# The swap of halves in a rotary embedding: from two half-height multiplies on VectorE to two ScalarE copies and one full multiply

## The chip, the cores and the metric

The kernel runs on one core of a Trainium2 chip. The metric is device time in microseconds (us) from one launch to its end. The core has five engines that run side by side: TensorE (PE) multiplies matrices, VectorE (DVE) and ScalarE (ACT) work element by element, GpSimd (POOL) here only issues DMAs, and SyncE (SP) issues most of the other DMAs. Each engine takes its instructions in a fixed order, which is decided when the program is built, and waits at each until its inputs are there.

## The reference

One layer of an encoder is applied to two sequences, x_sample with 1024 tokens and x_prompt with 512, each with 2048 channels, all in float32. The input is normalised and multiplied by one combined weight w_in. Of the columns of the result, three groups of 1024 feed a convolution path (value, gate inside the path, output gate); the rest are eight query heads, two key heads and two value heads of 128 channels and the attention's output gate. Queries and keys get a rotary embedding:

```python
t1, t2 = tf[..., :half], tf[..., half:]
out = jnp.concatenate([t1 * cos - t2 * sin, t2 * cos + t1 * sin], axis=-1)
```

Here `half` is 64. Then come a windowed attention with a sink term, the convolution (31 taps per channel, layer norm, silu, a 1024x1024 weight), the gates, one output weight, the residual and a last normalisation.

## The kernel before

Activations lie with the channels on the 128 partitions and the tokens along the free dimension, so one head of a projection is a tile of 128 partitions x 512 tokens, and the two halves of a head are partitions 0 to 63 and 64 to 127. Every product is taken in three passes with a high and a low part of each operand (`parts`, L506 to L515: ACT writes the high part, DVE the rest).

The long sequence is projected by `Unit` (L94 on), which takes two head-wide columns and two halves of the tokens at once in seven products of twelve matmuls instead of eight (a Strassen-like scheme). ACT copies the accumulator (`tap`, L236), DVE adds (L257), and the second half of the 2048 input channels is added to the stored first half by an accumulating DMA, which POOL issues (`add_into`, L501) and which lands in an SBUF tile. When it has landed, a generator finishes the tile: for queries and keys that is `rotate` (L1076), which calls `rope` in place on the tile. These generators stand in a list (`later`, L266) and are run some products later by `turn_over` (L542), behind the ACT and DVE instructions issued last before them and with a raised priority. There are 10 heads of queries and keys and two halves of the tokens, so 20 calls. Queries stand beside an attention gate column (L1240), whose tile gets a multiply (L975) and a Silu (L983) shortly before.

The short sequence is projected by plain `Job`s (L386), 48 matmuls each into one of four accumulators. Its rotations read the accumulator in PSUM directly (`rotated`, L1073), as the evacuation of the job, with a raised priority and in the middle of the next job: 10 calls. At the same time the attention of the long sequence runs in a lane of generators, PE, DVE and ACT by turns (L1151 to L1213).

The convolution's taps (L1033, L1041) run on DVE in another lane of generators, which is advanced after each product at a rate; they fill DVE between the urgent work. The final order on each engine comes from a planner, which takes the instruction of highest priority that it believes to be ready at that time.

`rope` (L1061 to L1071) uses a scratch tile `b`, from one of two rings of four buffers in turn (`E`, L477), and the tables `cos` and `sin` (`rope_tables`, L1052; for the long sequence multiplied once with the norm's factor). The result is stored to DRAM by SP (L1074, L1078; in the profile L504).

Of the kernel before, what the change touches and what calls it, by code (L numbers as in the profile page):

```python
# [9 lines left out]
AF = mybir.ActivationFunctionType  # L10
ALU = mybir.AluOpType
# [734 lines left out]
class Sequence:  # L746
# [314 lines left out]
    def rope(self, acc, c, o=None):  # L1061
        e, nc = self.e, self.e.nc
        i = slice(c * W, c * W + W)
        if o is None:
            o = e.G()
        b = e.E()
        nc.vector.tensor_tensor(b[0:64], acc[64:128], self.sin[64:128, i], ALU.mult)
        nc.vector.tensor_tensor(b[64:128], acc[0:64], self.sin[0:64, i], ALU.mult)
        nc.vector.tensor_tensor(o, acc, self.cos[:, i], ALU.mult)
        nc.vector.tensor_tensor(o, o, b, ALU.add)  # L1070
        return o  # L1071
# [1105 lines left out]
```

## Time and profile before

| what | value |
|---|---|
| median of three runs | 2080.51 us (2079.76 to 2081.54) |
| profiled execution, first to last instruction | 2072.4 us |
| median minus that span | 8.1 us |
| PE busy | 2057.6 us (99%) |
| DVE busy | 1752.3 us (85%) |
| ACT busy | 1043.9 us (50%) |
| first rotation of the long sequence starts | 642.0 us |
| last one of the long sequence starts | 830.0 us |
| rotations of the short sequence start | 871.1 to 1021.6 us |
| calls of `rope` | 30 |

The profile is of one execution, and its times count from the first instruction. A row of a timeline holds the start, the duration, the engine, the line of the kernel, the operation, the tiles it writes and reads, and, in brackets, how long the engine stood idle before it and what ended that. A row of a group holds the number of instructions, then the busy time in us, the mean duration in ns, and the idle time ahead. PEld is the weight load of PE; an engine name with a q is that engine's queue issuing a DMA. Tiles go by their ring's name: g and u are the rings of `E`, a, b and c are accumulators in PSUM, hl the split weights, raw the weights as loaded.

### The profile page before, as it was taken

To read this page: it belongs to the slowest core of one execution; us is meant where nothing else is said; L and a number is where in the kernel's file an instruction comes from. 1 tells how busy PE (TensorE), PEld (TensorE's weight loads), DVE (VectorE), ACT (ScalarE), POOL (GpSimd) and SP (SyncE) were. 2 spreads that over 40 slices of the span, in tenths; PEclk is the share of its full clock that TensorE was granted. 3 is DMA by queue.
4 is the path that set the end of the run, shared out by engine and by line. 5 is a ranking of instruction groups with operands and counts; after the bars stand their busy time and mean duration, and the time that the engine had idled before them with its cause. 6 is when DMAs were issued, how large, how long until landed. Compare 5 with 4: busy or idle time off the path is not lost.

```text
span 2072.4 us, 27195 instructions
## 1 busy us (share of the span) xinstructions
PE 2057.6 (99%) x9256; PEld 1696.0 (82%) x9256; DVE 1752.3 (85%) x2873; ACT 1043.9 (50%) x1711; POOL 157.8 (8%) x240
## 2 busy tenths in 40 slices
PE   9999999999999999999999999999999999999998
PEld 8888888888888888788888888888888888888886
DVE  8767899998899999889866877767799978998877
ACT  7485445333464443644455777336454343454454
POOL 0111111101111112100000000000000111100000
PEclk9999999999999999999999999999999999999999
DMA  8888786864577776954455555997789899678897
GB/s 295 312 299 254 197 222 220 292 214 154 193 242 192 178 173 172 290 169 154 159 172 187 176 183 182 317 331 235 246 288 302 281 317 297 206 249 297 290 334 275
DMA packets 242300, 494.56 MB, mean 239 GB/s; under 512 B 23664, under 2 KB 84464, under 8 KB 242160
## 3 DMA queue, kind: packets, MB, share of 16 engines
q1 hardware_dynamic: 216352, 428.83, 61.6%
q0 software_dynamic: 24512, 61.88, 12.1%
q10 hardware_dynamic: 1296, 2.11, 0.3%
q8 instruction: 72, 1.18, 0.2%
q14 instruction: 68, 0.56, 0.1%
HBM read 331.77 MB, written 160.96 MB: 238 GB/s over the span
## 4 chain that ended last, share of the span: by engine, by line
PE 52%; issue 7%; DVE 4%; DMA 2%; POOL 1%; ACT 1%; POOLq 0%; ACTq 0%; SPq 0%; DVEq 0%
PE a L670 14%; PE c L670 7%; PE b L670 7%; PE a L207 7%; PE c L207 3%; PE s L1168 2%; PE pv L1197 2%; PE s L1851 2%; PE a L1851 2%; PE b L207 1%; PE pt L1202 1%; DVE hl L511 1%; PE pt L1851 1%; PE pv L1851 1%; POOL u L501 1%
## 5 line engine op out<-in xcount | busy, mean ns | idle before, releaser
L207 PE MATMUL a<-t,hl 128*128 128x512 f32 x2640 | 633.1, 390 | 2.0 <-ACT g L236 1.3
L207 PEld LDWEIGHTS a<-t,hl 128*128 128x128 f32 x2640 | 493.2, 188 | 109.5 <-ACT g L236 2.6
L510 ACT ACTIVATE hl<-raw 128x1024 fp32r<-128x1024 f32 (+3 forms) x334 | 296.1, 890 | 375.3 <-PE c L207 90.6
L511 DVE TENSOR_TENSOR hl<-raw,hl 128x1024 fp32r<-128x1024 f32 (+3 forms) x334 | 337.9, 1012 | 143.6 <-ACT hl L510 142.0
L670 PE MATMUL a<-t,hl 128*128 128x512 f32 x1344 | 325.8, 393 | 0.0
L207 PE MATMUL c<-t,hl 128*128 128x512 f32 x1320 | 319.2, 389 | 0.0
L670 PEld LDWEIGHTS a<-t,hl 128*128 128x128 f32 x1344 | 248.9, 188 | 50.2
L207 PEld LDWEIGHTS c<-t,hl 128*128 128x128 f32 x1320 | 247.4, 188 | 51.5 <-DVE u L304 0.2
L1041 DVE SCALAR_TENSOR_TENSOR f<-f,c_w_dw,f 128x512 f32<-128x512 f32 x248 | 173.3, 745 | 0.3
L670 PE MATMUL b<-t,hl 128*128 128x512 f32 x672 | 163.6, 393 | 1.3 <-DVE t L515 0.8
L1004 DVE SCALAR_TENSOR_TENSOR f<-f,c_w_dw,f 128x512 f32<-128x512 f32 x232 | 163.7, 745 | 1.0 <-ACT f L999 0.9
L670 PE MATMUL c<-t,hl 128*128 128x512 f32 x672 | 164.4, 393 | 0.0
L207 PE MATMUL b<-t,hl 128*128 128x512 f32 x660 | 159.8, 389 | 0.0
L670 PEld LDWEIGHTS b<-t,hl 128*128 128x128 f32 x672 | 124.6, 188 | 27.4 <-DVE t L515 1.1
L670 PEld LDWEIGHTS c<-t,hl 128*128 128x128 f32 x672 | 124.7, 188 | 24.7
L207 PEld LDWEIGHTS b<-t,hl 128*128 128x128 f32 x660 | 123.7, 188 | 25.6
L1033 DVE SCALAR_TENSOR_TENSOR f<-f,w_both,f 128x512 f32<-128x512 f32 x120 | 89.8, 748 | 2.3 <-ACT f L1027 0.3
L236 ACT ACTIVATE u<-a 128x512 f32<-128x512 f32 x82 | 48.7, 594 | 69.7 <-PE a L207 66.9
L236 ACT ACTIVATE g<-a 128x512 f32<-128x512 f32 x78 | 46.4, 595 | 70.0 <-PE a L207 65.1
L1182 ACT ACTIVATE p<-p,tiny 128x384 f32<-128x384 f32 (+1 forms) x96 | 54.5, 570 | 44.1 <-DVE tiny L1179 25.2
L510 ACT ACTIVATE a<-pt 128x512 fp32r<-128x512 f32 x64 | 38.0, 593 | 63.9 <-PE pt L1202 63.6
L418 ACT ACTIVATE hl<-raw 128x1024 fp32r<-128x1024 f32 x43 | 45.4, 1056 | 47.1 <-PE a L670 18.7
(354 smaller groups left out, 2713.0 us busy)
## 6 DMA issues: line engine op xcount, KB each, us to landing
raw<-w_in SPq DMA_DIRECT2D x170, 512.0 KB, 5.2
raw<-w_out SPq DMA_DIRECT2D x31, 512.0 KB, 5.3
raw<-w_pw SPq DMA_DIRECT2D x24, 512.0 KB, 4.2
wsum_P<-raw SPq DMA_DIRECT2D x47, 256.0 KB, 3.5
raw<-wsum_P SPq DMA_DIRECT2D x18, 512.0 KB, 4.7
f<-x_s SPq DMA_DIRECT2D x16, 512.0 KB, 8.7
g<-wsum_P SPq DMA_DIRECT2D x28, 256.0 KB, 4.4
a<-sum_S SPq DMA_DIRECT2D x24, 256.0 KB, 6.7
```

The lines of the kernel that those rows point to most:

```text
L207: nc.tensor.matmul(acc, hl[:, l, o, j, :], toks[j][:, r], start=name in FRESH and j == 0 and q == 0, stop=name in LAST and j == HALF - 1 a ...
L236: nc.scalar.activation(t, bank, AF.Copy)
L418: e.nc.scalar.activation(t[:, 0], raw, AF.Copy)
L510: nc.scalar.activation(hi, x, AF.Copy)
L511: nc.vector.tensor_tensor(lo, x, hi.bitcast(F32), ALU.subtract)
L670: nc.tensor.matmul(job.acc[0], hl[:, l, kk // HALF, kk % HALF, :], r, start=i == 0 and p == 0, stop=i == nk - 1 and p == 2,)
L1004: nc.vector.scalar_tensor_tensor(t, h[:, j : j + T], w(j), t, ALU.mult, ALU.add)
L1033: nc.vector.scalar_tensor_tensor(m0, odd[:, j : j + H], both(j), m0, ALU.mult, ALU.add)
L1041: nc.vector.scalar_tensor_tensor(out, d[:, j : j + H], w(2 * j + k), out if j else m0, ALU.mult, ALU.add)
L1168: nc.tensor.matmul(ps[:, 0:n], qs[:, x, h], k[y][:, keys], start=p == 0, stop=p == 2)
L1182: nc.scalar.activation(p[:, 0:n], p[:, 0:n], AF.Exp, bias=nm[:, h : h + 1], accum_out=l[:, h : h + 1])
L1851: nc.tensor.matmul(acc[t], self.toks[name, m][:, x, i, t * P : (t + 1) * P], parts[i][l].rearrange("p a b -> p (a b)"), start=fresh and fi ...
```

## The change

The swapped product `b` was written by two DVE multiplies, each from one half of the tile to the other half of `b`. Now two ACT copies write the swapped halves, and one DVE multiply of all 128 partitions multiplies `b` in place by the sine table. Since the multiplier now is indexed by the output's half and not by the input's, the table's signs are exchanged. The cosine multiply and the addition stay.

```diff
         b = e.E()
-        nc.vector.tensor_tensor(b[0:64], acc[64:128], self.sin[64:128, i], ALU.mult)
-        nc.vector.tensor_tensor(b[64:128], acc[0:64], self.sin[0:64, i], ALU.mult)
+        nc.scalar.activation(b[0:64], acc[64:128], AF.Copy)
+        nc.scalar.activation(b[64:128], acc[0:64], AF.Copy)
+        nc.vector.tensor_tensor(b, b, self.sin[:, i], ALU.mult)
         nc.vector.tensor_tensor(o, acc, self.cos[:, i], ALU.mult)
         nc.vector.tensor_tensor(o, o, b, ALU.add)
...
-    arrays["sin"] = np.concatenate([sin, -sin])
+    arrays["sin"] = np.concatenate([-sin, sin])
```

## The prediction

> **What bounds the kernel now.** I read the page first: its span and the busy shares.
>
> ```profile
> span 2072.4 us, 27195 instructions
> PE 2057.6 (99%) x9256; PEld 1696.0 (82%) x9256; DVE 1752.3 (85%) x2873; ACT 1043.9 (50%) x1711; POOL 157.8 (8%) x240
> ```
>
> TensorE is without an instruction for 2072.4 - 2057.6 = 14.8 us in all, VectorE (DVE) for 320 us, ScalarE (ACT) for more than half of the span. A shared average can hide a stage, so next came busy time by stretches: one without rotary work, the 20 rotations of the long sequence (640 to 835 us), and the 10 of the short one (835 to 1026 us). The columns are PE, weight loads, DVE, ACT, POOL, each with its count of instructions, then clock, DMA share and GB/s.
>
> ```profile
> 400.00:620.00 220.00, 219.81 (x970) 181.69 (x969) 199.65 (x298) 95.09 (x145) 26.02 (x45) 1.00 0.63 209
> 640.00:835.00 195.00, 194.62 (x862) 159.71 (x861) 190.67 (x285) 78.14 (x122) 35.04 (x40) 1.00 0.71 175
> 835.00:1026.00 191.00, 188.59 (x875) 154.46 (x874) 171.60 (x302) 97.94 (x177) 6.08 (x7) 1.00 0.60 193
> ```
>
> Two things stand here. In 640 to 835 DVE has only 195.00 - 190.67 = 4.33 us left, so it is nearly full where the change acts. Yet PE misses only 0.38 us there, and its instructions come at 195.00 / 862 = 0.226 us, as they do with DVE at 91% (220.00 / 970 = 0.227 us). PE sets the pace; DVE is full because filler work (the convolution taps) is put into it. What the change can win on PE while it acts is at most 0.38 + 2.41 = 2.8 us of idle time.
>
> **What the change removes on DVE.** Grouped by shape within 640 to 835, then all calls of the first multiply by stretch:
>
> ```profile
> L1067 DVE TENSOR_TENSOR g<-u,f 64x512 f32<-64x512 f32 x10 | 6.9, 687 | 0.8 <-DMA u<-part_q 0.6
> L1068 DVE TENSOR_TENSOR g<-u,f 64x512 f32<-64x512 f32 x10 | 6.9, 685 | 0.1
> L1070 DVE TENSOR_TENSOR u<-u,g 128x512 f32<-128x512 f32 x10 | 6.9, 687 | 0.1
> ```
>
> ```profile
> 640.00:835.00 195.00, 13.73 (x20) 1.00 0.71 175
> 835.00:1026.00 191.00, 6.93 (x10) 1.00 0.60 193
> ```
>
> A multiply of 64 partitions takes 0.687 us, as long as one of 128 (0.687 us). Two go and one comes: 0.69 us of busy time per rotation, 20.6 us over 30. What an engine really pays is the distance between starts, and there the old pair costs more:
>
> ```profile
> 660.18 0.68 DVE L1070 TENSOR_TENSOR g<-g,u 128x512 f32<-128x512 f32 x1
> 660.79 0.68 DVE L257 TENSOR_TENSOR u<-g,u 128x512 f32<-128x512 f32 x1
> 661.39 0.68 DVE L143 TENSOR_TENSOR p<-raw,raw 128x512 f32<-128x512 f32 x1
> 662.11 0.69 DVE L1067 TENSOR_TENSOR g<-u,f 64x512 f32<-64x512 f32 x1
> 662.81 0.69 DVE L1068 TENSOR_TENSOR g<-u,f 64x512 f32<-64x512 f32 x1
> 663.52 0.69 DVE L257 TENSOR_TENSOR g<-c,g 128x512 f32<-128x512 f32 x1
> ```
>
> Full operations follow each other at 0.60 us. The one ahead of the pair, the first and the second half take 0.72, 0.70 and 0.71 us. From L143 to the next L257 pass 2.13 us; with one full multiply in place of the halves it would be 2 x 0.60 = 1.20. DVE wins 0.93 us per rotation: 18.6 us in 640 to 835, 9.3 us behind it, 27.9 us in all.
>
> The Trainium skill names the cause in "VectorE: DVE Perf Modes", section "Two Vector instructions with no wait between them": an operation whose input or output starts in another group of 32 partitions than the last one's is held until every earlier one has finished. The trace agrees (0.70 to 0.72 against 0.60 us). By durations alone the sum on DVE would be 20.6 us, by the rule 27.9 us; PE's time is the same by both.
>
> Worth on PE: bounds 0 and -2.8 us (all idle of both stretches). I take -0.2 us, half of the 0.38 us, because the cover of DVE's work is PE itself and the 2.41 us lie at the change of sequences (below), after the last long rotation.
>
> **What it adds on ACT.** No copy of 64 partitions is in the trace. Nearest are full 128x512 operations in the same stretch (from SBUF, SBUF, PSUM), and two back to back:
>
> ```profile
> L510 ACT ACTIVATE hl<-raw 128x512 fp32r<-128x512 f32 x20 | 12.5, 624 | 45.7 <-DVE raw L143 43.6 <-PE c L207 2.2
> L983 ACT ACTIVATE g<-g 128x512 f32<-128x512 f32 x9 | 5.7, 633 | 14.1 <-DVE g L975 14.1
> L236 ACT ACTIVATE u<-a 128x512 f32<-128x512 f32 x20 | 11.8, 589 | 5.6 <-PE a L207 5.4
> ```
>
> ```profile
> 848.03 0.63 ACT L983 ACTIVATE g<-g 128x512 f32<-128x512 f32 x1
> 848.55 0.62 ACT L983 ACTIVATE u<-u 128x512 f32<-128x512 f32 x1
> ```
>
> Lower bound per copy: half of 0.589, 0.29 us; upper: 0.633 + 0.10 if it were held as DVE's halves are, 0.73 us. I take 0.62, since halving the partitions won nothing on DVE. A pair then fills 0.52 + 0.62 = 1.14 us (bounds 0.6 and 1.5); 30 pairs are 34 us. ACT has 116.9 us free in the first stretch, 93.1 in the second. The question is what stands behind the copies on ACT. That is the evacuation of PE's accumulator (L236), and PE waits for it. The rotations come in pairs, one per half of the tokens. The last first-of-a-pair:
>
> ```profile
> 829.74 1.05 ACT L510 ACTIVATE hl<-raw 128x1024 fp32r<-128x1024 f32 x1
> 830.02 0.69 DVE L1067 TENSOR_TENSOR g<-u,f 64x512 f32<-64x512 f32 x1
> 830.96 2.88 PE L207 MATMUL c<-t,hl 128*128 128x512 f32 x12
> 831.15 0.60 ACT L236 ACTIVATE g<-a 128x512 f32<-128x512 f32 x1 [0.37 <-PE a L207]
> 833.67 0.61 PE L207 MATMUL a<-t,hl 128*128 128x512 f32 x2
> ```
>
> The copies can start at 830.7, when ACT is done with L510, and end near 831.9 at worst ahead of the evacuation, which then ends at 832.5 instead of 831.75. PE wants that bank at 833.67: 1.2 of 1.9 us of room are left, cost 0. Without this room each such rotation would cost up to 0.75 us. At the second of a pair ACT is empty; this is the evacuation's neighbour for the rotation that starts at 796.63:
>
> ```profile
> 798.86 0.63 ACT L510 ACTIVATE hl<-raw 128x512 fp32r<-128x512 f32 x1 [6.31 <-DVE raw L143]
> ```
>
> 6.31 us of idle ACT take 1.14 us at no cost. The copies also take over DVE's wait for the projection's accumulating DMA:
>
> ```profile
> DVE u L1067 <- DMA g<-part_q: 1.1, 1, 1.1
> DVE g L1067 <- DMA u<-part_q: 0.6, 1, 0.6
> ```
>
> Both are late second ones; 1.1 + 1.14 us is under the 6.31 us. In the short sequence the copies read PSUM (0.59 each) amid the attention's round trips, where PE's weight loads already wait shortly (620 to 1035 us):
>
> ```profile
> PEld pv L1197 <- DVE a L511: 1.3, 5, 0.4
> PEld pt L1202 <- ACT p L1189: 0.8, 3, 0.3
> ```
>
> That is 2.1 us in 8 waits, 0.26 each. Bounds for ten rotations: 0, and 10 x 1.14 = 11.4 us if each copy pair stood whole in a round trip. ACT is half empty there (97.94 of 191.00), so I take three of ten with one more such wait: +0.8 us.
>
> **What moves.** The full multiply waits for both copies, and the in-place cosine multiply of the long sequence too. Behind them on DVE the planner has other ready work, as it has now (L1041 stands between the parts of the rotation). The result was ready 3.5 us after the start (830.02 to 832.83 + 0.69); 1.14 + 0.60 + 0.60 + 0.69 is 3.0 us, plus handing over. So the store on SP's queue isn't later, and the weight load behind it has 6 us:
>
> ```profile
> 820.17 0.32 SPq L504 DMA_DIRECT2D q_d<-u  x1
> 826.31 0.33 SPq L127 DMA_DIRECT2D raw<-w_in  x1
> ```
>
> The tables' sign change is in the input and costs nothing; no DMA is added.
>
> **Sum.** -0.2 + 0 + 0.8 = +0.6 us on the profiled 2072.4, so 2073.0. The median of the runs is 2080.51, 8.1 above the span; with that, 2081.1 us.
>
> **Rivals.** *ACT blocks the evacuations* (slower). The trace has the mechanism once:
>
> ```profile
> 840.59 1.95 ACT L514 ACTIVATE t<-a,c_norm_g 128x512 fp32r<-128x512 f32 x3
> 842.44 0.58 ACT L236 ACTIVATE g<-a 128x512 f32<-128x512 f32 x1
> 843.07 3.01 PE L207 MATMUL a<-t,hl 128*128 128x512 f32 x12 [1.07 <-ACT g L236]
> ```
>
> 1.95 us of ACT ahead of an evacuation cost PE 1.07 us. Two copies behind one L510 are 1.14 + 1.05 = 2.19 us. It decides from four rotations on (4 x 1.07 = 4.3 us); with 8 of 20 it is +8.6, 2089 us. Against it: the 1.2 us of room above.
>
> *DVE's relief shows* (faster). DVE is 98% busy for 195 us, and if PE followed it, 18.6 + 9.3 us would go: 2052.6 us. Against it are the equal 0.226 and 0.227 us per PE instruction at 98 and 91% DVE. The Trainium skill, "Perfetto Trace Analysis", section "Identifying the Most-Contended Engine", distrusts PE's matmul busy share and would look at the weight loads, here 82%, which makes DVE the engine to relieve; the even spacing speaks against it here.
>
> *DVE stands waiting for the copies.* If nothing fills the 1.14 us, each rotation costs DVE 1.14 - 0.93 = 0.21 us more; 20 of them, 4.2 us, fit into the 4.33 us it has. Then the relief isn't there, and the time stays: 2080.5 to 2081.
>
> **Chances.** Forecast 0.65; ACT blocks 0.18; DVE's relief shows 0.07; DVE waits 0.10. The measurement can tell about 0.2%, 4.2 us. Within it fall the forecast and the last rival: same 0.75; faster 0.07; slower 0.18. The forecast's own range is -2.8 to +3 us, 2077.7 to 2083.5. For 8 in 10 I widen it upward into the blocking case, to 2088, and down to 2077; the planner orders everything anew, and moves waits of some tenths in later stages.
>
> **What would show it.** Right: DVE busy falls by about 20 us and what stands around the rotation on DVE follows at 0.60 us; copies take 0.6 us; PE's instructions in 640 to 835 still come at 0.226 us; PE's idle there stays under 1.5 us. Wrong: PE rows in these stretches with waits of 0.5 us and more on L236 or on L510, L1182 and L1189; ACT idle ahead of a copy with an evacuation ready behind it; or PE's spacing under 0.226 us, which would mean that DVE set it.

## The result, and the profile after

| what | value |
|---|---|
| changed kernel, median of 22 runs | 2077.62 us (2073.97 to 2081.12) |
| kernel before, 22 runs beside them | 2081.26 us (2076.56 to 2086.94) |
| ratio | 0.9981, 95% interval 0.9974 to 0.9988 |
| difference | -4.0 us (-5.4 to -2.5), from 0.0019 x 2081 |
| forecast | 2081.1 us, range 2077 to 2088 |

The change makes the kernel 0.19% faster. That is a gain, though a hair inside the 0.2% that the prediction called no change. The time lies in the range; the sign of the forecast (+0.6 us) is wrong.

The page of the changed kernel, its span and busy shares:

```profile
span 2077.4 us, 27223 instructions
PE 2060.1 (99%) x9256; PEld 1697.9 (82%) x9256; DVE 1728.4 (83%) x2843; ACT 1081.8 (52%) x1771; POOL 157.9 (8%) x240
```

This is a trap: the span after is 5.0 us *longer* than the 2072.4 us of before, though 22 runs say that the kernel is faster. The profiled execution of the changed kernel took 2079.13 us in all, 1.7 us more than its span, so about 1.7 us lie outside a span. The first profile of before would then be one of about 2074.1 us, below all 22 timed runs of that kernel. Both kernels were therefore profiled once more, for the comparisons below: the spans are then 2079.4 us (before) and 2073.8 us (after). One execution differs from the next by as much as the change is worth or more (7.0 us before, 3.6 us after), so a difference of two spans says nothing here. What two profiles of a kernel agree on can be used.

The stretches of the prediction, after (PE, weight loads, DVE, ACT, POOL, then clock, DMA share and GB/s):

```profile
640.00:835.00 195.00, 195.00 (x869) 160.99 (x868) 177.55 (x267) 104.78 (x162) 35.01 (x41) 1.00 0.74 177
835.00:1026.00 191.00, 189.20 (x879) 155.75 (x878) 163.76 (x291) 110.62 (x198) 6.00 (x7) 1.00 0.60 193
```

In the long sequence's rotations the stretch holds 869 instructions of PE where it held 862, and PE misses nothing. DVE's busy time falls by 190.67 - 177.55 = 13.1 us, which is 20 operations of 0.687 us (13.7 us). It is not free, though. The two longest of DVE's waits in this stretch after the change (total us, times, longest):

```profile
DVE u L1069 <- ACT u L1068: 7.1, 9, 1.6
DVE g L1069 <- ACT g L1068: 6.3, 4, 2.6
```

It stands 13.4 us at the new multiply (L1069 after the change), waiting for the second copy. Busy and waiting together are 177.55 + 13.4 = 191.0 us, as much as the 190.67 us before. The relief is eaten on DVE, and yet PE gains.

The copies, by shape from 640 to 1026 us, and one pair in the timeline (here and in the timelines below, rows of other work are left out):

```profile
L1068 ACT ACTIVATE g<-u 64x512 f32<-64x512 f32 x10 | 6.3, 632 | 0.1
...
L1068 ACT ACTIVATE g<-a 64x512 f32<-64x512 f32 x4 | 2.4, 592 | 0.1
```

```profile
789.36 0.63 ACT L1067 ACTIVATE g<-u 64x512 f32<-64x512 f32 x1
790.01 0.63 ACT L1068 ACTIVATE g<-u 64x512 f32<-64x512 f32 x1
790.66 0.60 ACT L236 ACTIVATE u<-c 128x512 f32<-128x512 f32 x1
790.67 0.69 DVE L1069 TENSOR_TENSOR g<-g,f 128x512 f32<-128x512 f32 x1
```

A copy of 64 partitions takes 0.632 us (0.592 in the short sequence, which reads PSUM). The two start 0.65 us apart, where two full operations before (848.03 and 848.55) started 0.52 apart. The last row but one is an evacuation that starts right behind the pair.

**Where PE's gain is.** The order of instructions on every engine is the same in both kernels up to about 641 us and again from about 1027 us. A steady difference must come from between. PE's own order is the same up to 938 us, so the same matmuls are compared. In all profiles I counted PE's instructions in 640 to 835 us: with the old pair 862 and 856 (two profiles of before), with the copies 869 and 868. The rows of the second profiles, before and after:

```profile
640.00:835.00 195.00, 194.15 (x856) 158.03 (x855) 189.16 (x283) 77.42 (x122) 35.03 (x40) 1.00 0.71 172
```

```profile
640.00:835.00 195.00, 195.00 (x868) 160.93 (x867) 177.91 (x269) 105.21 (x162) 35.69 (x41) 1.00 0.74 178
```

Of this count, 9.5 instructions more at 195 / 868.5 = 0.2245 us each are 2.1 us. PE's wait at 841 us (row 843.07 of the prediction) shrinks as well; PE's waits for the evacuation from 640 to 870 us, before and after:

```profile
PE a L207 <- ACT g L236: 1.3, 2, 1.1
...
PE a L207 <- ACT u L236: 0.2, 1, 0.2
```

```profile
...
PE a L207 <- ACT g L236: 0.3, 1, 0.3
```

The one at 841 us was 1.07 and 1.09 us in the two profiles of before, 0.35 and 0 in the two of after: on the mean some 0.9 us. Together 3.0 us, inside the interval of the difference. The way between two matmuls that are the same in all kernels, near 622 and near 843 us, gives as much: against the first profile of before, its second one takes 1.5 us more, the two of after 2.0 and 2.5 us less, 3.0 us on the mean.

**The mechanism.** At 826 us the same work stands in both timelines. Before:

```profile
825.00 2.88 PE L207 MATMUL c<-t,hl 128*128 128x512 f32 x12
826.20 0.68 DVE L975 TENSOR_TENSOR u<-u,f 128x512 f32<-128x512 f32 x1
826.91 0.64 ACT L983 ACTIVATE u<-u 128x512 f32<-128x512 f32 x1 [2.10 <-DVE u L975]
827.45 0.58 ACT L236 ACTIVATE u<-a 128x512 f32<-128x512 f32 x1
828.09 1.19 PE L207 MATMUL a<-t,hl 128*128 128x512 f32 x4 [0.20 <-ACT u L236]
```

After:

```profile
825.47 2.88 PE L207 MATMUL c<-t,hl 128*128 128x512 f32 x12
825.59 0.69 DVE L975 TENSOR_TENSOR u<-u,f 128x512 f32<-128x512 f32 x1
826.31 0.63 ACT L983 ACTIVATE u<-u 128x512 f32<-128x512 f32 x1 [2.15 <-DVE u L975]
826.85 0.58 ACT L236 ACTIVATE u<-a 128x512 f32<-128x512 f32 x1
828.19 2.88 PE L207 MATMUL a<-t,hl 128*128 128x512 f32 x12
```

Read it from the bottom. PE wants bank a for the next product and waits for its evacuation (L236). ACT would have been free for it, idle 2.10 us, but its order has a Silu (L983) in front, which waits for the gate's multiply on DVE (L975). DVE started that multiply 1.20 us after PE had started the product c; after the change, 0.12 us. From L975 it is 0.71 us to L983, 0.54 to L236 and 0.64 to PE, 1.89 us together, and a product that nothing holds starts 2.72 us after the one before it (825.47 to 828.19). So PE starts late when L975 starts more than about 0.83 us into the product. In 640 to 835 us all of PE's waits for an evacuation in before are of this kind: two in the first profile, three in the second, with L975 1.17 to 1.40 us into the product. The starts of the matmuls follow the sum closely: with L975 0.99, 1.17, 1.20 and 1.40 us in, the next product is 0.16, 0.34, 0.36 and 0.56 us late (the first of these leaves no idle time in the profile, so it is in no list of waits). In none of the profiles kept of this case is such a product late where L975 comes before 0.83 us; in the two of the changed kernel 0.12 us is the latest. The engine named in PE's wait is ACT; the late one is DVE.

The wait at 841 us has the same root by another way. ACT's chain in front of that evacuation (L510, L510, L983, L236, L514) begins behind DVE's first pass over new weights (L143). Before and after:

```profile
836.44 0.69 DVE L143 TENSOR_TENSOR raw<-raw,raw 128x512 f32<-128x512 f32 x1
...
837.25 0.63 ACT L510 ACTIVATE hl<-raw 128x512 fp32r<-128x512 f32 x1 [5.49 <-PE a L207]
```

```profile
835.67 0.68 DVE L143 TENSOR_TENSOR raw<-raw,raw 128x512 f32<-128x512 f32 x1
...
836.47 0.64 ACT L510 ACTIVATE hl<-raw 128x512 fp32r<-128x512 f32 x1 [4.36 <-DVE raw L143]
```

DVE comes 0.77 us earlier (835.67 for 836.44), L510 as much, and PE's wait is 0.72 us shorter (0.35 for 1.07). ACT had been idle for 5.49 us. The row names PE as what ended that; L510 starts 0.12 us after DVE's L143 ends, which is the later of the two.

### The profile page after: what moved, and what is told of

Its sections match the earlier page's. It is cut to its first block, busy times and chain, and to the rows that moved or that the text cites. A ratio compares the mean times of both kernels' runs of the same rounds, so it can differ in the third digit from the quotient of the medians.

```text
span 2077.4 us, 27223 instructions
## 1 busy us (share of the span) xinstructions
PE 2060.1 (99%) x9256; PEld 1697.9 (82%) x9256; DVE 1728.4 (83%) x2843; ACT 1081.8 (52%) x1771; POOL 157.9 (8%) x240
## 3 DMA queue, kind: packets, MB, share of 16 engines
q0 software_dynamic: 24512, 61.88, 12.5%
## 4 chain that ended last, share of the span: by engine, by line
PE 73%; issue 8%; DMA 8%; DVE 7%; ACT 2%; POOL 1%; SPq 0%; ACTq 0%; POOLq 0%; DVEq 0%
PE a L207 21%; PE a L670 13%; PE c L207 10%; PE b L670 6%; PE c L670 6%; PE b L207 5%; PE s L1169 2%; PE pv L1198 2%; PE a L1852 2%; PE s L207 2%; DVE hl L511 2%; PE pt L1203 1%; PE s L1852 1%; DVE t L511 1%; DMA p<-y_d 1%
## 5 line engine op out<-in xcount | busy, mean ns | idle before, releaser
L510 ACT ACTIVATE hl<-raw 128x1024 fp32r<-128x1024 f32 (+3 forms) x334 | 296.8, 889 | 314.4 <-PE c L207 88.1
L236 ACT ACTIVATE u<-a 128x512 f32<-128x512 f32 x82 | 48.8, 595 | 77.3 <-PE a L207 70.6
L236 ACT ACTIVATE g<-a 128x512 f32<-128x512 f32 x78 | 46.5, 596 | 78.5 <-PE a L207 68.5
L510 ACT ACTIVATE a<-pt 128x512 fp32r<-128x512 f32 x64 | 38.0, 593 | 64.6 <-PE pt L1203 64.4
L285 POOL DMA_DIRECT2D g<-xT_s x16 | 8.8, 551 | 743.1 <-DMA att_d<-u 669.0
```

The costliest lines, as they stand in the source:

```text
L236: nc.scalar.activation(t, bank, AF.Copy)
L510: nc.scalar.activation(hi, x, AF.Copy)
```

## The experiments

The theory: *DVE runs full and in order in 640 to 835 us, so its work for ACT (L975, L143) comes late, and the lateness reaches PE through ACT's order (L983 or L510, then L236).* Rivals: the gain comes from the short sequence; from the copies as such (a new order, ACT's work); or from later stages.

**The long sequence alone, the short one alone.** `self.s` is 0 in the long sequence; the second kernel has 1 in its place.

```diff
+        if self.s == 0:
             nc.scalar.activation(b[0:64], acc[64:128], AF.Copy)
             nc.scalar.activation(b[64:128], acc[0:64], AF.Copy)
             nc.vector.tensor_tensor(b, b, self.sin[:, i], ALU.mult)
+        else:
+            nc.vector.tensor_tensor(b[0:64], acc[64:128], self.sin[64:128, i], ALU.mult)
+            nc.vector.tensor_tensor(b[64:128], acc[0:64], self.sin[0:64, i], ALU.mult)
         nc.vector.tensor_tensor(o, acc, self.cos[:, i], ALU.mult)
-        nc.vector.tensor_tensor(o, o, b, ALU.add)
+        nc.vector.tensor_tensor(o, o, b, ALU.add if self.s == 0 else ALU.subtract)
```

> The 20 rotations of the long sequence use the two ACT copies and the full multiply, the 10 of the short one keep the two half multiplies (the sign of the table is taken up by a subtraction). Theory A, DVE's relief in 640 to 835 us lets the Silu and the evacuations behind it start earlier, so that PE's small waits there and at the change of sequences shrink: most of the gain, 2.0 to 4.0 us under the kernel before. Theory B, the gain comes from the short sequence, where PE's order of attention and projection matmuls is changed: within 1 us of the kernel before. Theory C, both parts add: about 2 us.

> Only the 10 rotations of the short sequence use the copies. Theory A: within 1 us of the kernel before, or slower by my predicted 0.8 us. Theory B: 2.5 to 4 us faster. Theory C: about 2 us faster.

Measured: long alone 0.9992 (0.9984 to 1.0001), short alone 0.9997 (0.9988 to 1.0006). By time neither is told from no change; long alone is at -1.7 us, less than the 2.0 us that the theory asked for. By PE's count they part; the long one, then the short one:

```profile
640.00:835.00 195.00, 195.00 (x867) 160.69 (x866) 177.10 (x268) 104.66 (x162) 35.13 (x41) 1.00 0.74 177
```

```profile
640.00:835.00 195.00, 194.16 (x858) 158.44 (x857) 189.44 (x284) 77.70 (x122) 35.05 (x40) 1.00 0.71 172
```

867 goes with the changed kernel, 858 with before. The first kernel also leaves the order of PE and POOL wholly as it was, so its count needs no new order of the matmuls. In the short sequence nothing is seen; its attention's stretch before and after:

```profile
870.00:1026.00 156.00, 156.00 (x737) 128.85 (x736) 142.76 (x260) 71.93 (x137) 0.00 (x0) 1.00 0.51 168
```

```profile
870.00:1026.00 156.00, 156.00 (x738) 129.43 (x737) 135.06 (x250) 84.04 (x157) 0.00 (x0) 1.00 0.52 169
```

**DVE's relief without copies, and copies without relief.** The first kernel leaves the swap out of the computation (one full multiply of the unswapped tile); the second makes the copies and then overwrites them with the old multiplies, reading the tile as before.

```diff
-        nc.vector.tensor_tensor(b[0:64], acc[64:128], self.sin[64:128, i], ALU.mult)
-        nc.vector.tensor_tensor(b[64:128], acc[0:64], self.sin[0:64, i], ALU.mult)
+        nc.vector.tensor_tensor(b, acc, self.sin[:, i], ALU.mult)
```

```diff
+        nc.scalar.activation(b[0:64], acc[64:128], AF.Copy)
+        nc.scalar.activation(b[64:128], acc[0:64], AF.Copy)
         nc.vector.tensor_tensor(b[0:64], acc[64:128], self.sin[64:128, i], ALU.mult)
         nc.vector.tensor_tensor(b[64:128], acc[0:64], self.sin[0:64, i], ALU.mult)
```

> The swap is left out: one full DVE multiply of the unswapped tile takes the place of the two half multiplies, and there are no ACT copies. So DVE has the same relief, and ACT no extra work. Theory A: at least the gain of the change, 3.5 to 5 us, since nothing is added on ACT. If the gain came from the new places of the work on ACT and not from DVE: 0 to 1 us.

> The two ACT copies are made and then overwritten by the two old half multiplies: ACT's cost and DVE's wait for ACT without the relief of DVE. Theory A: no gain, 0 to 3 us slower than the kernel before, and PE's waits in 640 to 870 us as before or longer. If the copies' placing made the gain: 2 to 4 us faster.

Measured: relief alone 0.9984 (0.9974 to 0.9993), -3.3 us; copies alone 1.0022 (1.0013 to 1.0032), +4.6 us. Their rows, in this order:

```profile
640.00:835.00 195.00, 195.00 (x869) 161.42 (x868) 180.50 (x272) 80.38 (x123) 35.67 (x41) 1.00 0.76 182
```

```profile
640.00:835.00 195.00, 193.06 (x840) 154.42 (x839) 185.16 (x277) 98.75 (x156) 34.17 (x39) 1.00 0.70 169
```

The relief alone gives a gain that is not told from that of the change, with no copy in the kernel. The copies by themselves cost: 859 - 840 = 19 instructions of 0.227 us, 4.3 us, about what the time shows. The place is the same; a wait in the kernel with both, in its timeline (rows between are left out):

```profile
775.07 0.68 DVE L975 TENSOR_TENSOR g<-g,f 128x512 f32<-128x512 f32 x1
...
775.79 0.63 ACT L983 ACTIVATE g<-g 128x512 f32<-128x512 f32 x1 [2.39 <-DVE g L975]
...
776.33 0.58 ACT L236 ACTIVATE g<-a 128x512 f32<-128x512 f32 x1
...
776.96 0.50 PE L207 MATMUL a<-t,hl 128*128 128x512 f32 x1 [0.45 <-ACT g L236]
```

ACT had idled 2.39 us for L975. Of PE's six waits for an evacuation in this kernel's stretch, three are of this kind (0.19, 0.45 and 0.19 us), one stands behind an L510 that waited for DVE (0.57). In the other two (0.23 and 0.22) a Silu that came late from DVE is followed by the two copies, and only then by the evacuation: there the copies do hold PE, 1.30 us of ACT in front of L236, but only where ACT had idled for DVE just before. DVE stands 7.2 us at the first of the old multiplies in this stretch, waiting for the copies. Four of the six waits go back to work of DVE that came late, so that this standing is most of what the copies cost is likely; it was not separated from the rest of the new order.

**How much relief is needed.** Two full multiplies in place of the halves, the first one overwritten; the swap is left out here too. DVE has the old number of operations and loses only the longer distance between starts: by the prediction's rows 2.13 - 3 x 0.60 = 0.33 us per rotation instead of 0.93.

```diff
-        nc.vector.tensor_tensor(b[0:64], acc[64:128], self.sin[64:128, i], ALU.mult)
-        nc.vector.tensor_tensor(b[64:128], acc[0:64], self.sin[0:64, i], ALU.mult)
+        nc.vector.tensor_tensor(b, acc, self.sin[:, i], ALU.mult)
+        nc.vector.tensor_tensor(b, acc, self.sin[:, i], ALU.mult)
```

> Two full multiplies without the swap take the place of the two half multiplies (the swap is left out; the first one's result is overwritten), nothing on ACT. By the spacing of the traces DVE then wins only what the halves pay for their form, 2.13 - 3 x 0.60 = 0.33 us per rotation, 6.6 us in the long sequence. Theory A, DVE's occupation counts: a part of the gain, 0.5 to 2.5 us, some of the waits behind L236 left. If it takes the whole relief of 18.6 us to move anything: within 0.5 us of the kernel before.

Measured: 0.9987 (0.9978 to 0.9995), -2.7 us.

```profile
640.00:835.00 195.00, 195.00 (x869) 161.42 (x868) 189.42 (x288) 80.38 (x122) 34.96 (x40) 1.00 0.73 177
```

DVE is as busy as before (189.42 us), and PE's count is 869 all the same. That is more than the theory expected (a part of the gain, some waits left). By this count a third of the relief buys all that is to be had in the stretch: once the waits are gone, PE is busy 195.00 of 195.00 us. Of the wait at 841 us 0.7 us is left. This also shows that DVE's *busy* time is no measure of how late it runs. The 0.33 us are in no busy column; they are in the distance between starts. The Trainium skill's rule in "VectorE: DVE Perf Modes", section "Two Vector instructions with no wait between them", on operations that are held because they start in another group of 32 partitions, thus has a price on PE here: taking the held operations away won these 2.7 us (1.0 to 4.6), with DVE's order planned anew.

**DVE's load changed by other work.** The rate at which convolution taps fill DVE in this stretch (third value), lowered in the kernel before, raised in the changed one, then lowered in it.

```diff
-RATES = (0.4, 0.6, 0.3, 1.0, 0.5)
+RATES = (0.4, 0.6, 0.2, 1.0, 0.5)
```

> The old half multiplies stay; the lane that feeds the convolution's taps to DVE runs at 0.2 instead of 0.3 in the stage of the long sequence's rotations, which takes some 20 to 27 us of filler off DVE there (it is done later). Theory A, any relief of DVE there does it: PE's waits behind L236 at 712, 808 and 827 us vanish and PE is 1 to 2.5 us earlier at the end of that stage; over the whole time 1 to 4 us faster, if the taps find room later. If it were the swap's own form that counts: the waits stay and the time is the same.

> The changed kernel with the lane of the taps at 0.4 instead of 0.3 in that stage: the filler takes back DVE's relief. Theory A: PE's waits behind L236 between 640 and 850 us are back, 2 to 5 us more than in the changed kernel, so as fast as the kernel before or slower. If DVE's occupation doesn't count: as the changed kernel, 3 to 4 us faster than the kernel before.

> The changed kernel with the lane of the taps at 0.2 in that stage, both reliefs together. Theory A: no wait behind L236 in 640 to 840 us is left to be won, so within 1.5 us of the changed kernel, 3 to 5 us faster than the kernel before; what would show more is the change of sequences (841 to 868 us).

Measured: before with 0.2, 0.9990 (0.9981 to 0.9999); after with 0.4, 1.0032 (1.0019 to 1.0044); after with 0.2, 0.9971 (0.9960 to 0.9981), median 2075.17 us. The rows in this order:

```profile
640.00:835.00 195.00, 195.00 (x869) 161.47 (x868) 178.63 (x265) 81.34 (x124) 35.62 (x41) 1.00 0.73 178
```

```profile
640.00:835.00 195.00, 192.03 (x844) 156.06 (x843) 182.31 (x277) 100.60 (x157) 33.91 (x39) 1.00 0.71 169
```

```profile
640.00:835.00 195.00, 195.00 (x869) 161.42 (x868) 163.10 (x246) 104.93 (x163) 35.68 (x41) 1.00 0.74 177
```

The kernel before needs no new rotary embedding to reach 869: fewer taps do it. The changed one falls to 844 when the taps come back. There DVE is less busy than in the kernel before (182.31 us for 190.67), but it stands 10.7 us at the new multiply. With fewer taps it keeps 869 and has the lowest median of all kernels run. It beats the kernel before. Against the changed kernel its interval overlaps (0.9974 to 0.9988), and its profile has no gain in this stretch over after's, so that it beats that one too is likely, not shown.

**How far this goes.** The changed kernel with 0.1, and the long sequence alone with 0.2:

```diff
-RATES = (0.4, 0.6, 0.3, 1.0, 0.5)
+RATES = (0.4, 0.6, 0.1, 1.0, 0.5)
```

> The changed kernel with the lane of the taps at 0.1 in the stage of the long rotations. Theory A says that nothing is left to be won there (no wait behind L236 is left at 0.2), while more taps have to find room behind 870 us: as fast as at 0.2 or 1 to 3 us slower, so 2 to 6 us under the kernel before.

> Copies in the long sequence alone, half multiplies in the short one, and the lane of the taps at 0.2. Theory A, only the long sequence counts: as fast as the changed kernel with that lane, 4.5 to 7 us under the kernel before. If the short sequence's copies help too (0.3 us in its stretch of the profile): 0.3 to 1 us slower than that.

Measured: 1.0022 (1.0010 to 1.0035), which is 4.6 us slower than before where 2 to 6 us faster were expected, and 0.9983 (0.9973 to 0.9992). Taps that aren't done here are done later. With 0.1 the stretch behind the rotations and the two after it read:

```profile
1026.00:1300.00 274.00, 274.00 (x1295) 225.99 (x1294) 217.65 (x414) 180.95 (x307) 0.00 (x0) 1.00 0.57 183
1300.00:1600.00 300.00, 294.84 (x1344) 242.98 (x1343) 235.21 (x391) 134.47 (x225) 7.75 (x14) 1.00 0.83 278
1600.00:1900.00 300.00, 295.79 (x1319) 242.67 (x1318) 267.47 (x422) 133.65 (x215) 27.46 (x50) 1.00 0.82 272
```

The second profile of the changed kernel with 0.3, in the middle one of them:

```profile
1300.00:1600.00 300.00, 299.62 (x1370) 248.22 (x1369) 239.99 (x400) 139.62 (x232) 7.75 (x14) 1.00 0.85 287
```

1344 against 1370. This count varies by itself (1356 in the other profile of after, 1371 and 1358 in the two of before), but 1344 is below all four. PE's waits from 1300 to 1900 us come to 9.3 us, against 0.8 to 2.8 us in those four. The load on DVE moves: from 1026 to 1300 us it is busy 217.65 us, against 192.3 us in the first profiles of both kernels. PE loses nothing there; why it waits more behind it was not followed. So 0.2 is between two losses, but the cause of the second is not shown.

The long sequence alone with 0.2 isn't told from the changed kernel with 0.2 by time (their intervals overlap), so no worth of the short sequence's part is shown. The profile has a difference, though, at the change of sequences. A row of PE in the long sequence alone with 0.2, and the 6 us from 870 us on:

```profile
869.63 0.50 PE L670 MATMUL b<-t,hl 128*128 128x512 f32 x1 [1.75 <-ACT t L514]
870.00:876.00 6.00, 5.20 (x13) 4.00 (x13) 5.91 (x9) 3.05 (x4) 0.00 (x0) 0.51 0.62 176
```

PE waits 1.75 us for its operand (L514), which ACT makes late because an L510 further ahead in its order had waited 2.75 us for a DMA (q_d). In the kernel before with 0.2 the same wait is 2.2 us, in the changed kernel with 0.2 it is 0.6 us. So part of what PE wins in the rotations can be lost again there: in the kernel before with 0.2 the way from the matmul near 622 us is 2.65 us shorter than in the first profile of before up to the one near 843, and only 0.8 us up to the one near 870; in long alone it is 1.5 and 0.7 us. These are single profiles.

**Before and after once more,** for a second profile of each:

> The kernel before once more, for a second profile of it. The time is that of the kernel before, within 1.5 us. Theory A: the same waits behind L236 at 700 to 850 us as in its first profile, 1.5 to 3.5 us together; the first profile was below every timed run, so the stages behind 1300 us should hold some 2 to 6 us more of waits here.

> The changed kernel once more, for a second profile and to stand beside the others of this call. The time is 2 to 5 us under the kernel before. Theory A: as in its first profile, no wait behind L236 between 640 and 840 us, and one of some 0.5 us near 841 us.

Measured: 0.9999 (0.9990 to 1.0007) and 0.9988 (0.9980 to 0.9997). The gain holds in this set too, -2.5 us (-4.2 to -0.6); what both sets allow is -2.5 to -4.2 us. The stretch from 640 to 870 us accounts for some 3.0 of it.

What stays open: the planner orders DVE's work anew in each kernel, so L975 and L143 move both because DVE has less to do and because other work stands in front of it. The kernels with one full or two full multiplies and the one with fewer taps reach the same count by different orders, which speaks for the load; a kernel with one order and another load wasn't run.

## Why the prediction was wrong, step by step

**What bounds the kernel: half right.** "PE sets the pace" and DVE is full with filler, yes. But filler is not free where urgent work queues behind it on an engine that runs in order.

**DVE's relief on PE, -0.2 us: this is the step that failed.** It measures -3.0 us in 640 to 870 us, against a bound of "at most 0.38 + 2.41 = 2.8 us of idle time" for both stretches. Three readings were off:

- *Idle time undercounts a wait.* The product with the wait of 0.20 us idle starts 3.09 us after the one before it (825.00 to 828.09); without a wait it is 2.72 us (12 x 0.227). The loss is 0.37 us, because a matmul's row lasts 0.39 us with a modelled end, while the next one can start after 0.227 us. The second matmul behind the wait follows at 0.335 us, another 0.11 us lost. Two profiles of before have 0.38 and 0.85 us of idle time in 640 to 835, and lack 6.5 and 12.5 instructions against after's 868.5: 1.5 and 2.8 us. The count of instructions holds three to four times the loss that the idle column shows. In the first profile the three late starts (0.16, 0.34 and 0.36 us) and 0.11 us behind each come to 1.2 of the 1.5 us; the rest was not traced.
- *0.226 against 0.227 us per PE instruction compared unlike things.* The stretch from 400 to 620 holds matmuls of 512 columns alone, 0.227 us from start to start; 640 to 835 also holds 16 short ones of 128 columns (L1102), 0.109 us apart. The mean spacing with no waits in this stretch is 195 / 868.5 = 0.2245 us, not 0.227, and 195 / 862 = 0.226 already held the loss. The prediction named "PE's spacing under 0.226 us" as the sign that DVE had set it. That sign came.
- *The waits on L236 were not followed back.* The row 843.07 was read as "1.95 us of ACT ahead of an evacuation" and made the price of a rival. Those 1.95 us of ACT stand there after the change too; what shrank the wait was DVE's L143, some 6 us earlier.

**The distance between starts on DVE, 0.93 us per rotation:** right in kind, and the kernel with two full multiplies shows that even its 0.33 us count. DVE's busy time fell by 1752.3 - 1728.4 = 23.9 us over the whole span, where 20.6 us were worked out by durations.

**The copies on ACT, cost 0:** right. A copy takes 0.632 us (0.62 was taken). A pair takes 0.65 + 0.63 = 1.28 us from its start to its end, not 1.14, because the copies don't overlap as full operations do; within the bounds of 0.6 and 1.5. PE has no wait for an evacuation left in 640 to 835 us. The rival that ACT blocks the evacuations did not come. It is real, though: in the kernel with copies and no relief it shows twice (0.23 and 0.22 us), behind a Silu that DVE had made late.

**The short sequence, +0.8 us:** 737 and 738 instructions in 870 to 1026, short alone 0.9997. It is 0 as far as it can be told.

**The rival "DVE stands waiting":** it happened, 13.4 us or 0.67 per rotation (0.21 were priced), and still its conclusion failed. "Then the relief isn't there, and the time stays" holds for DVE's total. But the waits fell where nothing urgent stood behind L1069, and the relief where L975 did.

**The rival "DVE's relief shows", 2052.6 us:** right in its mechanism, seven times too large (27.9 us for 4.0). PE doesn't follow DVE step for step over 195 us; it meets it at a handful of places, and the gain ends when those are gone. The Trainium skill's "Perfetto Trace Analysis", section "Identifying the Most-Contended Engine", which distrusts PE's matmul busy share, was on the right side: 99% busy hid the loss. The weight loads' share, which it recommends (160.99 against 159.71 us here), moves with the count and would have shown it no earlier.

**8.1 us around the span:** about 1.7 of them lie outside the span; the other 6.4 were an execution that ran faster than usual. The forecast from the median wasn't hurt by it.

## What to carry to other kernels

Where an engine runs in order and is nearly full in a stretch, ask of each wait of the bounding engine what stood *ahead* of the named instruction on its engine, and what that one waited for: the late one may be an engine further back. Value such waits by the count of instructions that the bounding engine starts in a fixed stretch, over two profiles of each kernel, and not by its idle time. Expect a gain up to the point where those waits are gone, none beyond it, and look where the moved load lands.

## What the runs showed of the hardware

**A PE wait can cost more than itself.** In the changed kernel with more taps PE waits 2.55 us at 629 us. Its row, and then the stretches around it:

```profile
631.86 4.59 PE L207 MATMUL a<-t,hl 128*128 128x512 f32 x12 [2.55 <-ACT u L236]
```

```profile
629.00:632.00 3.00, 0.45 (x3) 0.15 (x2) 3.00 (x6) 1.69 (x4) 0.87 (x1) 1.00 0.69 187
632.00:636.00 4.00, 4.00 (x11) 3.17 (x12) 4.00 (x6) 2.31 (x4) 0.86 (x1) 0.57 0.97 270
636.00:640.00 4.00, 4.00 (x19) 3.30 (x19) 3.44 (x6) 2.43 (x5) 0.00 (x0) 1.00 1.02 298
```

The granted clock falls to 0.57 for the 4 us after the wait, and twelve matmuls take 4.59 us instead of 2.88: another 1.7 us. The Trainium skill, "TensorE: Matmul & The Clock Gate", section "HAM oscillation — how this bites in real kernels", warns of gaps over about 3.4 us; here 2.55 us were enough. The length of the wait doesn't settle it: the clock also fell behind the 1.75 us shown above (one of 0.81 us follows right behind it), and it stayed at 1.00 behind waits of 3.28 and 2.41 us (at 1408 and 1712 us, the changed kernel with 0.1). Near the end of the kernel it falls in some executions with no wait of PE ahead of it, behind 16 matmuls of one column (L701); before and after, from 1912.5 us:

```profile
1912.50:1917.00 4.50, 4.50 (x21) 3.72 (x21) 3.54 (x9) 2.93 (x5) 0.00 (x0) 1.00 0.69 256
```

```profile
1912.50:1917.00 4.50, 4.44 (x14) 3.32 (x14) 4.16 (x10) 2.87 (x5) 0.00 (x0) 0.66 0.98 341
```

21 instructions at clock 1.00, 14 at 0.66. The second profile of the changed kernel has no such fall, so this is one of the ways in which one profile of a kernel differs from the next.

**Half-height copies on ACT** start 0.64 to 0.65 us apart, where two full ones (Silu) in this kernel overlap and start 0.52 apart. That resembles what DVE does with its half-height multiplies (0.70 against 0.60); whether the starting partition is the cause was not tested.
